# Pads in three tile pools move transposed activations and inner feed-forward tiles to 224 modulo 256 bytes

## The chip, the cores and the metric

The kernel runs on one core of one Trainium2 chip. The metric is the device time of one execution in microseconds (us), given as a median over runs. Where a time comes from the profile, it is from one profiled execution, and its times count from the start of its span.

## The reference

The program is two transformer stacks of two layers each, one after the other, on 512 tokens with 1024 features (the first stack has 256 context tokens besides). All of it is in float32. Cut to what takes the time:

```python
def sq_relu_mlp(h, w1, w2):                       # first stack, 1024 -> 4096 -> 1024
    return jnp.square(jax.nn.relu(h @ w1)) @ w2
...
def swiglu_half(x, w1, w3, w2):                   # second stack, 1024 -> 2816 -> 1024
    return 0.5 * ((jax.nn.silu(x @ w1) * (x @ w3)) @ w2)
...
    for layer in range(DEPTH):                    # first stack
        y_c, y_l = ab_mixer(...) if layer % 2 == 0 else c_mixer(...)
        x = x + mod_l[:, :, 2] * y_l
        x = x + mod_l[:, :, 5] * sq_relu_mlp(modulate(x, norm2_g[layer], mod_l, 3), mlp_w1[layer], mlp_w2[layer])
...
    for l in range(DEPTH):                        # second stack
        x = layer_norm(ALPHA * x + swiglu_half(x, ffn1_w1[l], ffn1_w3[l], ffn1_w2[l]), ln1_g[l], ln1_b[l])
        h = x @ w_in[l]
        mix = jnp.concatenate([out_a, out_b, out_c], axis=-1) @ w_out[l]
        x = layer_norm(ALPHA * x + mix, ln2_g[l], ln2_b[l])
        x = layer_norm(ALPHA * x + swiglu_half(x, ffn2_w1[l], ffn2_w3[l], ffn2_w2[l]), ln3_g[l], ln3_b[l])
```

`ab_mixer`, `c_mixer` and the three branches `out_a`, `out_b`, `out_c` are attention and recurrences; they begin and end with dense products over 1024 features.

## The kernel before

Every dense product is made of three matmuls (`mm3`, line 154): operands are split into a high and a low part (names ending in H and L, or `wh` and `wl` for weights), and high by high, high by low and low by high are added up in PSUM. Each of them goes through `mm` (line 142). A matmul has a moving operand, whose columns stream through the array, and a stationary one of 128 columns, which a weight load puts there before. In a row of the profile `ps<-hH,wh` the first name after the arrow is the moving operand and the second the stationary one; `128*128 128x512` is the shape of the stationary operand and that of the output.

There are three patterns of product.

- Activations move over stationary weights, 8 row blocks and 24 matmuls for each 128 output features. This is `genA` (line 1624), the first product of `mlp` (line 1151) and that of `ffn` (line 1823). The moving tiles are `hH`, `hL` (512 tokens) and in the first stack `hcH`, `hcL` (256 context tokens): activations transposed to features by tokens. At the start of each feed-forward the first pieces run on 256 tokens at a time. Outside the mixers this makes, by the loops, 3840 matmuls of 512 columns in the four feed-forwards of the second stack (22 feature tiles by 2 weights by 24, less four tiles that run in halves) and 1440 in the two of the first.
- Weights move over stationary activations: `genB` (line 1638) and `genP` (line 497) in the mixers, with `hH`, `hL`, `hcH`, `hcL` as the stationary tiles.
- Weights move over stationary inner tiles of a feed-forward: `genP` in `mlp` with the tiles called `hid`, and `gen2` (line 1797) in `ffn` with `hidH`, `hidL`.

Weights come by DMA into `wf` (two buffers of 1 MB), are split by ScalarE (`wh`) and VectorE (`wl`) into four buffers each, one piece ahead of use, and used in the order of the list `specs`. In the feed-forwards nothing else stands on TensorE's queue but transposes of `x`; in the mixers generators of small work are woven between the dense matmuls by a rough clock (`service`, `drive`), and this order does not know where a tile lies.

Tiles are laid out from two ends of each partition. `pool` (line 193) opens a pool on the left, on top of what is open there; `right` (line 190) does it on the right. On the left lie `const`, then `hT` (`hH`, `hL`), then `sm1` (small tiles of the first stack) with `hTc` (`hcH`, `hcL`) and the pools of layer and feed-forward above it; for the second stack `sm2` takes the place of `sm1`, with `hidf` (`sl`, `hidH`, `hidL`) above. The weight buffers lie on the right. In the built program the tiles start at these bytes of a partition:

| tiles | byte before | mod 256 | mod 512 |
|---|---|---|---|
| `wh`, `wl` (all buffers) | 180192 and up, 4096 apart | 224 | 480 |
| `hH`, `hL` | 21952, 38336 | 192 | 448 |
| `hcH`, `hcL` | 62752, 70944 | 32 | 288 |
| `hid` of `mlp` | 87328 and up, 3072 apart | 32 | 288 |
| `hidH`, `hidL` of `ffn` | 69344 and up, 2048 apart | 224 | 224 |
| `kTH`, `kTL`, `vH`, `vL`, `pt` of the first stack's layer 1 | 82208, 88352, 94496, 100640, 134432 and up | 32 | 288 |

A matmul of 512 columns takes a slice that starts a multiple of 512 bytes further on, so the residues are those of the operands too. Only the pieces of weights that are 272 or 288 columns wide have slices at other residues.

Of the kernel before, what the change touches and what calls it, by code (L numbers as in the profile page):

```python
# [7 lines left out]
F32 = mybir.dt.float32  # L8
# [4 lines left out]
PSUM = bass.MemoryType.PSUM  # L13
# [11 lines left out]
VF = 1.0  # L25
# order of emission in the mixers: priorities of chains, backlog they may see, order of the projections
MIX = {"lim": 12.0, "marg": 0.15, "slow": "", "ord": "UVQZ", "invy": (5, 8, 10, 12, 14) + tuple(range(16, 31)), "invw": 6.0, "rgw": 0, "rgp": 1,
# [6 lines left out]
PVX = 1  # L34
N6, NQ, N5, N5B = 9, 4, 13, 15


# [10 lines left out]
class Lane:  # L48
    """an engine whose calls are passed on and added to a rough clock, for the order of emission"""

# [52 lines left out]
class Slots:  # L103
    """tiles handed out and given back in the order of emission"""

# [10 lines left out]
class Net:  # L116
# [10 lines left out]

# [1 line left out]
    def ps(self):  # L129
# [60 lines left out]
    def right(self, es, name, bufs=1):  # L190
        return es.enter_context(self.tc.tile_pool(name=name, bufs=bufs, side="right", reuse_waits="tile"))

    def pool(self, es, name, **kw):
        return es.enter_context(self.tc.tile_pool(name=name, bufs=1, side="left", reuse_waits="tile", **kw))

# [1 line left out]
    def run(self):  # L197
# [38 lines left out]

    # ================= first block =================
    def slots(self, pool, n, size, tag):
        return Slots([pool.tile([128, size], F32, name=f"{tag}{i}") for i in range(n)])

    def tok(self, t):
        """features by tokens of tile t: context 0, 1, latents 2..5"""
        a, i = (self.hTc, t) if t < 2 else (self.hT, t - 2)
        c = slice(i * 128, i * 128 + 128)
        return a[0][:, :, c], a[1][:, :, c]
# [12 lines left out]
    def mild(self, i):  # L258
        """pieces whose low parts GpSimd takes: all of them, or the second half of each"""
        n = len(self.specs)  # L260
        if i in SLOW0:
            self.slow |= {n, n + 1}
        if -i - 1 in SLOW0:
            self.slow |= {-n, -n - 1}
# [44 lines left out]

    # feature blocks of layer 0's projection: columns, width, pieces of modulation weights between  # L310
    L0_proj = [
# [31 lines left out]

# [1 line left out]
    def ada_setup(self):  # L345
# [9 lines left out]
        p = self.pb.get()  # L355
# [8 lines left out]
        self.pb.put(p)  # L364
        # [layer, latents or context, part of the modulation, feature block]
        self.mod = cp.tile([128, 2, 2, 6, 8], F32, name="mod")
# [19 lines left out]
    def ada_first(self, c, n, f):  # L386
        """half c of shift and scale of the first norm, two row blocks"""
        r = 64 * c
        if n == 0:
            self.abanks[c] = self.pb.get()  # L390
        for k in range(2):
            for s in range(2):
                self.nc.tensor.matmul(self.abanks[c][r + 32 * s:r + 32 * s + 32, :], lhsT=self.sT[:, 2 * n + k, :], rhs=f[:, k, s, :],
                                      start=n + k == 0, stop=n == 3 and k == 1)
                self.pe(0.43)
        if n == 3:
            self.spawn(self.ch_first(c), 0)
# [44 lines left out]
    def gate_row(self, pool, l, i, r):  # L442
        """row of modulation i (2 or 5) for all partitions"""
        t = pool.tile([128, 1024], F32, name=f"gate{l}{i}{r}")
        j0 = (i % 2) * 2
        for j in range(2):
            q = 32 * (j0 + j) + r
            self.nc.sync.dma_start(t[:, j * 512:j * 512 + 512], self.mD[l][i // 2][q].partition_broadcast(128))
        return t

    def ch_mod(self, t, x, l, i, name, tm, keep=True):
        """modulated rms norm of token tile t, by features and split; x as two halves of 512"""
        r = 1 if t < 2 else 0
# [43 lines left out]
    def genP(self, tiles, width, evac, raw=(), lhs=None, gate=None):  # L497
        """token-major product with eight row blocks of weights, token tiles by pairs"""
        if lhs is None:
# [29 lines left out]

# [1 line left out]
    def layer0(self):  # L531
# [8 lines left out]
        vH, vL = kp.tile([128, 6, 128], F32R, name="vH"), kp.tile([128, 6, 128], F32R, name="vL")  # L540
        # keys of a head above themselves, and their low parts
        kD, kL = [kp.tile([128, 768], F32R, name=f"kD{g}") for g in range(2)], kp.tile([128, 768], F32R, name="kL")
# [9 lines left out]
        aTD = self.dp.tile([12, 512], F32, name="aTD")  # L552
        # norm of the inputs while the modulation is on its way
        self.tmes = ExitStack()
# [86 lines left out]

        # -- window attention
        def ch_rope(t, qk, v):
# [170 lines left out]
        def ch_switch():  # L814
            """room for the rest once the window attention is done"""
            yield [("pv", t, g) for t in range(6) for g in range(2)]
# [4 lines left out]

        # -- mLSTM
        def ch_gate():
# [312 lines left out]
    def gated(self, x, p, g):  # L1136
        """x += g * p"""
        s = self.tms.get()
        self.tms.put(s)
        self.tt(s, p, g, ALU.mult)  # L1140
        self.tt(x, x, s, ALU.add)
# [7 lines left out]

# [1 line left out]
    def mlp(self, l):  # L1151
# [81 lines left out]

# [1 line left out]
    def layer1(self):  # L1235
# [121 lines left out]
        def ch_rl(g, t, rl):  # L1357
            """rows of the reciprocal sums, for all partitions"""
            yield [("l", g, t, j) for j in range(4)] + [("ps", 1), ("SO", 1)]
# [78 lines left out]

# [1 line left out]
    def spawn(self, gen, prio=1):  # L1440
# [70 lines left out]

# [1 line left out]
    def spec(self, parts, a, b, cut, extra=False):  # L1513
        self.specs.append((parts, a, b, cut, extra))

    def specraw(self, q):
        """pieces of the modulation weights, used as they are"""
        for l, sc, k in q:
# [11 lines left out]
    def issue(self):  # L1530
        """loads for which a buffer is free"""
        while self.nr in self.released:
# [11 lines left out]
    def wsplit(self):  # L1544
        """closures that split the next piece"""
        i = self.ns
# [44 lines left out]
    def ahead(self):  # L1591
        """queue the split of the next weights"""
        self.issue()
# [19 lines left out]
    def specA(self, w, c0, n, extra=False):  # L1613
        """columns c0..c0+n of w, output features by 128"""
        for c in range(c0, c0 + n, 256):
# [8 lines left out]
    def genA(self, n, evac, more=(), take=tuple):  # L1624
        """n pieces of up to two output tiles of 128 features, 512 tokens; evac gives the bank back"""
        m = 0
# [11 lines left out]
    def genB(self, toks, width, evac):  # L1638
        """token-major, token tiles by pairs; evac gives the bank back"""
        w = [self.flat(self.W(1)), None]  # L1640
# [17 lines left out]

    # ================= second block =================
    def second_specs(self):  # L1660
# [80 lines left out]
    def g_layer_norm(self, y, n, eps, g, b):  # L1741
        """in place (y - mean) * rsqrt(var + eps) * g + b over n columns"""
        nc, sm = self.nc, self.sm
# [14 lines left out]
    def chain_T(self, t, x):  # L1758
        """x transposed and split into the columns of tile t of hT"""
        hH, hL = self.hT  # L1760
# [36 lines left out]
    def gen2(self, hs, epi):  # L1797
        """token-major product of the hidden tiles with 1024 columns"""
        n = len(hs)
# [98 lines left out]
    def mixers(self, l):  # L1898
# [12 lines left out]

        # conv weights by feature, spatial biases by token
        raw = self.sm.tile([128, 128], F32, tag="raw", name="raw", bufs=1)
# [52 lines left out]
        v4 = lambda x: x.rearrange("p (t h s) -> p t h s", t=4, h=8)  # L1966
        # small constants of the layer
        row = lambda nm, n: self.row(cs, I[nm + "_2"][l], n, nm)
# [21 lines left out]
        def ch_gdn_gates():  # L1990
# [30 lines left out]
            yield  # L2021
            # row of the cumulated gates of the chunk for its tokens
            gT = cs.tile([32, 128], F32, name="gd_T")
# [117 lines left out]
        def ch_inv():  # L2141
# [19 lines left out]
            yield P["invw"]  # L2161
            # E for the queries: keys up to the query of the same chunk
            for c in range(2):
# [18 lines left out]
        def head_out(out, ov, gate, nh, sq_, p, ev):  # L2182
            """rms norm per head of 64 of ov (PSUM), times gate"""
            sq = v2(sq_[:, :nh * 64], nh)
# [153 lines left out]
        def ch_prep():  # L2338
            """inverses and off-diagonal blocks of a tile as diagonal blocks"""
            Lc, Tc = T["Lc"], T["Tc"]  # L2340
# [353 lines left out]
```

## Time and profile before

| | |
|---|---|
| median of 3 runs | 3851.73 us (3850.28 to 3855.07) |
| span of the profiled execution | 3851.4 us; no other time is given for it |
| TensorE busy with matmuls | 3754.8 us, 97% |
| weight loads | 3016.6 us, beside the matmuls |
| VectorE, ScalarE, GpSimd busy | 1893.6, 1316.6 and 324.7 us |
| DMA engines' share | 30.4% |

The busy share of TensorE counts a matmul until its modelled end, and matmuls overlap; how fast they follow each other is read from the starts of rows of a timeline, or from the number of matmuls in a stretch.

### The profile page before, as it was taken

To read this page: it belongs to the slowest core of one execution; us is meant where nothing else is said; L and a number is where in the kernel's file an instruction comes from. 1 tells how busy PE (TensorE), PEld (TensorE's weight loads), DVE (VectorE), ACT (ScalarE), POOL (GpSimd) and SP (SyncE) were. 2 spreads that over 40 slices of the span, in tenths; PEclk is the share of its full clock that TensorE was granted. 3 is DMA by queue.
4 is the path that set the end of the run, shared out by engine and by line. 5 is a ranking of instruction groups with operands and counts; after the bars stand their busy time and mean duration, and the time that the engine had idled before them with its cause. 6 is when DMAs were issued, how large, how long until landed. Compare 5 with 4: busy or idle time off the path is not lost.

```text
span 3851.4 us, 46517 instructions
## 1 busy us (share of the span) xinstructions
PE 3754.8 (97%) x18941; PEld 3016.6 (78%) x18941; DVE 1893.6 (49%) x3367; ACT 1316.6 (34%) x2213; POOL 324.7 (8%) x283
## 2 busy tenths in 40 slices
PE   8999899999999999999999999999999999999998
PEld 5676777777877778878888878888888888778887
DVE  4646663333368654443334586433433355864334
ACT  4547441211345532232222543222222225423221
POOL 1202200000011000000000241000000002410000
PEclk9999999999999999999999999999999999999999
DMA  6214542433221122223323421232333234212222
GB/s 241 69 50 143 170 167 99 156 99 102 66 72 57 42 91 88 91 96 99 104 83 121 103 80 66 89 103 82 99 99 104 89 116 102 77 66 93 99 88 82
DMA packets 282310, 379.65 MB, mean 99 GB/s; under 512 B 49224, under 2 KB 207296, under 8 KB 276976
## 3 DMA queue, kind: packets, MB, share of 16 engines
q1 hardware_dynamic: 282096, 376.68, 30.4%
q8 instruction: 148, 2.42, 0.3%
q14 instruction: 66, 0.54, 0.0%
HBM read 359.50 MB, written 17.15 MB: 98 GB/s over the span
## 4 chain that ended last, share of the span: by engine, by line
PE 86%; DVE 7%; ACT 2%; POOL 1%; DMA 1%; issue 1%; SPq 0%; POOLq 0%; ACTq 0%; DVEq 0%
PE ps L142 82%; PE ps L151 3%; POOL r L81 1%; PE ps L380 1%; DVE wl L81 1%; DVE x L81 1%; DVE ui L81 1%; DVE ua L81 1%; DVE hL L81 1%; DVE mx L81 0%; DMA fa<-in_ada_w_dram 0%; DVE st L81 0%; ACT wh L81 0%; DVE tm L81 0%; DVE u L81 0%
## 5 line engine op out<-in xcount | busy, mean ns | idle before, releaser
L81 ACT ACTIVATE wh<-wf 128x1024 fp32r<-128x1024 f32 (+2 forms) x516 | 538.0, 1050 | 1493.7 <-PE ps L142 1261.4
L81 DVE TENSOR_TENSOR wl<-wf,wh 128x1024 fp32r<-128x1024 f32 (+2 forms) x496 | 600.3, 1216 | 809.2 <-ACT wh L81 808.8
L142 PE MATMUL ps<-hH,wh 128*128 128x512 f32 (+1 forms) x2336 | 885.6, 380 | 6.8 <-ACT hH L81 5.6
L142 PE MATMUL ps<-hL,wh 128*128 128x512 f32 (+1 forms) x2336 | 881.8, 378 | 0.0
L142 PE MATMUL ps<-hH,wl 128*128 128x512 f32 (+1 forms) x2336 | 881.0, 377 | 0.0
L142 PEld LDWEIGHTS ps<-hH,wh 128*128 128x128 f32 x2336 | 440.0, 189 | 108.0 <-issue 9.5
L142 PEld LDWEIGHTS ps<-hL,wh 128*128 128x128 f32 x2336 | 440.8, 189 | 88.8 <-DVE ss L81 1.7
L142 PEld LDWEIGHTS ps<-hH,wl 128*128 128x128 f32 x2336 | 440.7, 189 | 88.3
L142 PE MATMUL ps<-wh,hid 128*128 128x512 f32 x1280 | 405.1, 395 | 0.0
L81 POOL TENSOR_TENSOR r<-rs,mhalf 128x1 f32<-128x1 f32 (+4 forms) x112 | 135.9, 1215 | 2775.4 <-DVE rs L81 2760.7
L142 PE MATMUL ps<-wh,hH 128*128 128x512 f32 (+3 forms) x800 | 315.3, 395 | 3.8 <-ACT uc L81 2.1
L142 PE MATMUL ps<-wh,hL 128*128 128x512 f32 (+3 forms) x800 | 303.4, 380 | 4.5 <-DVE hL L81 4.2
L142 PE MATMUL ps<-wl,hH 128*128 128x512 f32 (+3 forms) x800 | 302.3, 379 | 1.0 <-DVE wl L81 1.0
L142 PEld LDWEIGHTS ps<-wh,hid 128*128 128x128 f32 x1280 | 239.6, 187 | 58.0
L142 PE MATMUL ps<-wh,hidH 128*128 128x512 f32 x704 | 274.3, 390 | 0.0
L142 PE MATMUL ps<-wl,hidH 128*128 128x512 f32 x704 | 274.0, 389 | 0.0
L142 PE MATMUL ps<-wh,hidL 128*128 128x512 f32 x704 | 273.9, 389 | 0.0
L142 PE MATMUL ps<-wl,hid 128*128 128x512 f32 x640 | 252.5, 394 | 0.0
L81 DVE SCALAR_TENSOR_TENSOR sl<-sl,ps 128x512 f32<-128x512 f32 x88 | 60.5, 687 | 259.7 <-PE ps L142 259.6
L142 PEld LDWEIGHTS ps<-wh,hH 128*128 128x128 f32 x800 | 152.1, 190 | 43.3 <-issue 5.8
L142 PEld LDWEIGHTS ps<-wh,hL 128*128 128x128 f32 x800 | 152.3, 190 | 36.9 <-DVE hL L81 7.4
L142 PEld LDWEIGHTS ps<-wl,hH 128*128 128x128 f32 x800 | 152.7, 191 | 26.2 <-DVE wl L81 1.5
(369 smaller groups left out, 4740.7 us busy)
## 6 DMA issues: line engine op xcount, KB each, us to landing
wf<-in_ffn_w_dram SPq DMA_DIRECT2D x120, 1024.0 KB
wf<-in_mlp_w_dram SPq DMA_DIRECT2D x64, 1024.0 KB
wf<-in_ada_w_dram SPq DMA_DIRECT2D x40, 1024.0 KB
wf<-in_w_in_dram SPq DMA_DIRECT2D x24, 1024.0 KB
wf<-in_ffn_w_dram SPq DMA_DIRECT2D x24, 512.0 KB
wf<-in_ab_w_in_dram SPq DMA_DIRECT2D x10, 1024.0 KB
fa<-in_ada_w_dram SPq DMA_DIRECT2D x16, 512.0 KB
wf<-in_w_out_dram SPq DMA_DIRECT2D x16, 512.0 KB
```

The source lines that it names most:

```text
L81: r = f(*a, **kw)
L142: self.nc.tensor.matmul(out, lhsT=l, rhs=r, start=start, stop=stop)
L151: self.nc.tensor.transpose(out, in_, self.ident)
L380: self.nc.tensor.matmul(self.abank[32 * j:32 * j + 32, :], lhsT=self.sT[:, k, :], rhs=f[:, 512 * j:512 * j + 512], start=k == 0, stop=k == 7)
```

## The change

A table `PAD` names three pools; when one of them is opened, a tile of so many bytes per partition is made first, and nothing writes or reads it. The rest of the diff takes out comments and docstrings.

```diff
+PAD = {'const': 32, 'sm1': 160, 'sm2': 224}
...
     def right(self, es, name, bufs=1):
-        return es.enter_context(self.tc.tile_pool(name=name, bufs=bufs, side="right", reuse_waits="tile"))
+        p = es.enter_context(self.tc.tile_pool(name=name, bufs=bufs, side="right", reuse_waits="tile"))
+        if name in PAD:
+            p.tile([128, PAD[name] // 4], F32, name="pad" + name, bufs=1)
+        return p
 
     def pool(self, es, name, **kw):
-        return es.enter_context(self.tc.tile_pool(name=name, bufs=1, side="left", reuse_waits="tile", **kw))
+        p = es.enter_context(self.tc.tile_pool(name=name, bufs=1, side="left", reuse_waits="tile", **kw))
+        if name in PAD:
+            p.tile([128, PAD[name] // 4], F32, name="pad" + name)
+        return p
```

All three pools are on the left. In the built program the tiles then start here:

| tiles | byte after | mod 256 | mod 512 |
|---|---|---|---|
| `wh`, `wl` | as before | 224 | 480 |
| `hH`, `hL` | 21984, 38368 | 224 | 480 |
| `hcH`, `hcL` | 62944, 71136 | 224 | 480 |
| `hid` of `mlp` | 87520 and up | 224 | 480 |
| `hidH`, `hidL` of `ffn` | 69600 and up | 224 | 480 |
| `kTH`, `kTL`, `vH`, `vL`, `pt` | 82400, 88544, 94688, 100832, 134624 and up | 224 | 480 |

The large working tiles of the second stack's mixers lie on the right and stay. Each engine has the same instructions in the same order as before, and the waits are the same but for one copy on GpSimd in the first stack's window attention, which waits for VectorE alone instead of VectorE and ScalarE. No DMA is added or moved.

## Rows read from the trace of the kernel before

**Rows 1.** The page: span, engines' busy time, and shares of the last chain.

```profile
span 3851.4 us, 46517 instructions
...
PE 3754.8 (97%) x18941; PEld 3016.6 (78%) x18941; DVE 1893.6 (49%) x3367; ACT 1316.6 (34%) x2213; POOL 324.7 (8%) x283
...
PE 86%; DVE 7%; ACT 2%; POOL 1%; DMA 1%; issue 1%; SPq 0%; POOLq 0%; ACTq 0%; DVEq 0%
```

**Rows 2.** Stretches: us, then busy (count) of PE, PEld, DVE, ACT, POOL; clock, DMA.

```profile
2620.00:2670.00 50.00, 50.00 (x216) 40.27 (x215) 17.47 (x19) 14.09 (x18) 0.00 (x0) 1.00 0.31 99
...
1594.00:1634.00 40.00, 40.00 (x173) 32.08 (x172) 17.23 (x21) 7.03 (x8) 0.00 (x0) 1.00 0.25 79
...
2280.00:2340.00 60.00, 56.33 (x459) 47.18 (x458) 39.32 (x67) 29.44 (x59) 20.48 (x18) 0.97 0.19 54
```

**Rows 3.** Timeline of TensorE: start and length in us; three pairs, nine matmuls apart.

```profile
2819.82 0.40 PE L142 MATMUL ps<-hL,wh 128*128 128x512 f32 x1
...
2821.92 0.40 PE L142 MATMUL ps<-hL,wh 128*128 128x512 f32 x1
...
1334.71 0.40 PE L142 MATMUL ps<-wl,hH 128*128 128x512 f32 x1
...
1336.81 0.39 PE L142 MATMUL ps<-wl,hH 128*128 128x512 f32 x1
...
2600.03 0.39 PE L142 MATMUL ps<-wl,hidH 128*128 128x512 f32 x1
...
2602.07 0.39 PE L142 MATMUL ps<-wl,hidH 128*128 128x512 f32 x1
```

**Rows 4.** Groups of matmuls by form: xcount, busy us, mean ns, idle before.

```profile
L142 PE MATMUL ps<-hH,wh 128*128 128x512 f32 x1952 | 776.7, 398 | 0.0
...
L142 PE MATMUL ps<-wh,hid 128*128 128x512 f32 x1280 | 405.1, 395 | 0.0
...
L142 PE MATMUL ps<-wh,hidH 128*128 128x512 f32 x704 | 274.3, 390 | 0.0
...
L142 PE MATMUL ps<-wh,hH 128*128 128x512 f32 x640 | 268.2, 420 | 3.8 <-ACT uc L81 2.1 <-ACT hH L81 1.4 <-DVE vL L81 0.3
...
L142 PE MATMUL ps<-hH,wh 128*128 128x256 f32 x384 | 108.9, 289 | 6.8 <-ACT hH L81 5.6 <-ACT wh L81 1.2
...
L142 PE MATMUL ps<-hcH,wh 128*128 128x256 f32 x256 | 72.9, 285 | 0.0
```

**Rows 5.** Timeline, layer 1 attention of the first stack: two rows twelve matmuls apart.

```profile
1172.22 0.51 PE L142 MATMUL ps<-kTH,hcH 128*128 128x384 f32 x2
...
1174.30 0.34 PE L142 MATMUL ps<-kTH,hcH 128*128 128x384 f32 x1
```

**Rows 6.** Timeline after three breaks in the stream: pairs eight, four and four matmuls apart.

```profile
3150.66 0.40 PE L142 MATMUL ps<-wl,hidH 128*128 128x512 f32 x1
...
3152.51 0.39 PE L142 MATMUL ps<-wh,hidH 128*128 128x512 f32 x1
...
3156.71 0.48 PE L142 MATMUL ps<-wh,hidH 128*128 128x512 f32 x1
...
3157.71 0.39 PE L142 MATMUL ps<-wl,hidH 128*128 128x512 f32 x1
...
1223.35 0.71 PE L142 MATMUL ps<-pt,vH 128*128 128x512 f32 x2
...
1224.35 0.33 PE L142 MATMUL ps<-kTH,hcL 128*128 128x384 f32 x1
```

**Rows 7.** Timeline, layer 0's feed-forward, context tokens: two pairs, 22 matmuls apart.

```profile
573.63 0.28 PE L142 MATMUL ps<-hcL,wh 128*128 128x256 f32 x1
...
576.13 0.28 PE L142 MATMUL ps<-hcH,wl 128*128 128x256 f32 x1
...
583.16 0.28 PE L142 MATMUL ps<-hcL,wh 128*128 128x256 f32 x1
...
585.75 0.28 PE L142 MATMUL ps<-hcH,wl 128*128 128x256 f32 x1
```

## The prediction

> **What bounds the kernel now.** I read the page first, then stretches, then single rows. The page shows TensorE busy for 3754.8 of 3851.4 us and on 86% of the chain that ended last; the next engine, VectorE, has 49% [rows 1]. So the end is set by how fast matmuls follow each other, and an edit that changes no instruction matters only if it changes that. The table of stretches is read next, for what else could hold TensorE: in 50 us of a feed-forward's first product TensorE is busy throughout at full clock (1.00, which is the 2.4 GHz level), VectorE for 17.47 us, ScalarE for 14.09 us, and DMA engines at 0.31 [rows 2]. Nothing there is near its limit, so matmuls that follow each other 3% faster would still be fed. In the mixers it is different: in 60 us of one, TensorE idles 3.7 us and VectorE and GpSimd are busier [rows 2]; time won there can turn into waiting.
>
> The length of a matmul's row (0.39 or 0.40 us) is not its price, since the next starts before it ends. The price is the distance of starts, and the timeline gives it. Activations `hH` over weights: nine matmuls in 2.10 us, 233.3 ns each. Weights over `hH`: the same 2.10 us. Weights over `hidH`: 2.04 us, 226.7 ns each [rows 3]. Weights over `hid`: 173 matmuls in 40 us; with one row's length added for the edge, 40.39/173 is 233.5 ns [rows 2]. All four are 128 by 128 by 512 at the same clock, without a wait. What sets the fast one apart by the table of places is that both its operands start at 224 modulo 256; in the others one of the two is at 224 and the other at 192 or 32. Which operand moves is not it by itself: weights move in the fast stream and in two slow ones.
>
> **The change part by part.** It adds no instruction, DMA or queue entry, and drops one wait of a GpSimd copy. What moves is the start of operands. After it `hH`, `hL`, `hcH`, `hcL` and `hid` stand at 224 like the weights, and `hidH`, `hidL` stay there. If equal residues are what makes 226.7 ns, each 512-column matmul of the slow patterns gains 6.6 ns. The sum, pattern by pattern:
>
> (a) Activations over weights outside the mixers: 3840 and 1440 by the loops, 5280 of the 3 x 1952 matmuls of that form [rows 4]. Weights over `hid`: 1280 rows, and half as many with the low weights, 1920. Together 7200 x 6.6 ns = 47.5 us. They run back to back, but after each break in the stream the distance needs some matmuls to settle: in the fast pattern eight matmuls after a break took 1.85 us, 231 ns each [rows 6]. There are some fifty such restarts in the first stack's feed-forwards (after each product of modulation weights and each change to 256 columns), at 8 x 4.6 ns each: 2 us off. 45.5 us.
>
> (b) In the mixers: 576 matmuls of activations over weights (5856 less 5280), and 3 x 640 of weights over `hH` [rows 4] with 384 over `hcH`: 2880. All of it at 6.6 ns would be 19 us, none of it 0. Small products are woven between them, so many run within eight matmuls of a break, where a good half of the difference is not yet there: half at 6.6 ns and half at 2 ns is 12.4 us. Some is given back where TensorE then waits for VectorE or ScalarE. I take 8 us.
>
> (c) 256-column matmuls: 3 x 384 over `hH` and 3 x 256 over `hcH` [rows 4], 1920. Here the trace has two levels at one and the same pair of residues (32 and 224): 22 matmuls in 2.50 us, 113.6 ns, and 22 in 2.59 us, 117.7 ns [rows 7]. So at this width the state of the stream decides too, and equal residues may give the lower level, the present one, or another some 2 ns above it. Bounds: 8 us gained, 4 us lost. I take 3 us gained.
>
> Sum: 45.5 + 8 + 3 = 56.5 us, so 3851.4 becomes 3795 us; the median of the runs, 3851.7, lies 0.3 us from the profiled span, so it moves alike. Bounds of this case: 47.5 + 19 + 8 = 74.5 us gained gives 3777; 45.5 + 0 - 4 gives 3810.
>
> Costs I put at nothing: the writers of the moved tiles (ScalarE and VectorE), which have room beside 50 us of TensorE [rows 2], so that even a few per cent more on each write would show only in the mixers; and the dropped wait, off TensorE's queue.
>
> [...] First the rows: in 50 us TensorE's weight loads take 40.27 us beside 50.00 us of matmuls [rows 2], so the next weights are being read nearly all the time that a moving operand is. [...]
>
> **The rivals.** *No change:* the fast stream is fast for another reason, say the order in which `gen2` goes through eight PSUM banks, three matmuls on each. Then every pattern keeps its distance: 3851 us. For it: in rows of 512 columns only this one program pattern runs at 226.7 ns for long. Against it: a stream from quite another place. In layer 1's attention twelve matmuls of 384 columns, both operands at 32, took 2.08 us, 173.3 ns each [rows 5]. From there to 226.7 ns is 53.4 ns for 128 columns more, 0.417 ns a column, one cycle of 2.4 GHz; both then have the same 13.3 ns on top of their columns, and 233.3 ns has 20. Equal residues gave the same small remainder in both. [...]
>
> *Slower:* what is good is not equality modulo 256 but a distance of 256 modulo 512. Before, `hidH` and `hidL` stand at 224 modulo 512 and the weights at 480; after, everything stands at 480. Then the slow patterns stay where they are, and `gen2`, 3 x 704 matmuls [rows 4], falls back to 233.3 ns: 2112 x 6.6 = 13.9 us, 3865 us. For it: in the trace of before, no long stream of 512 columns has both operands at the same residue modulo 512. Against it: the 384-column stream has (288 and 288), with the small remainder; and a 512-column stream at 288 and 288 restarts like `gen2`: four matmuls after a break take 1.00 us in both [rows 6]. It decides from the point where the feed-forwards' second products show over 230 ns.
>
> *Half of it:* the state needs weights as the moving operand, as in `gen2`. Then only `hid` (1920) and the mixers' weight-moving products gain, 12.7 us and about 6 us: 3833 us. Against it, again the 384-column stream, in which keys move and no weights.
>
> That something else becomes the bound I leave out as a case: DMA at 0.31 and VectorE at a third in the dense stretch [rows 2] would have to grow threefold.
>
> **How the numbers follow.** Equal residues help everywhere: 0.77, at 3777 to 3810, likeliest 3795. Half of it: 0.05, 3833. No change: 0.10, 3851. Slower: 0.08, 3865. The range goes from 3777 to 3835 and so holds the first two, 0.82. A measurement of this kernel can tell about 0.2%, 8 us, from no change. Faster by more than that: 0.82; within it: 0.10; slower: 0.08.
>
> **What would show it.** Right: in the profile after, nine matmuls of `hH` over weights take 2.04 us instead of 2.10 in the second stack's feed-forwards, likewise weights over `hid`, and `gen2` keeps 2.04; a feed-forward's first product of 528 matmuls takes 528 x 226.7 ns, 119.7 us, instead of 123; counts, order and clock are the same. Step (b) is right if the mixers together shorten by 6 to 12 us and TensorE's idle time there grows by a few. Step (c) is right if 22 matmuls of 256 columns take 2.50 us in most places. The prediction is wrong if the distance stays at 233.3 ns with both operands at 224, if `gen2` rises to 233, or if streams of equal residue settle at a third value.

## The result and the profile after

The changed kernel takes 3806.39 us (median of 4 runs, 3803.82 to 3811.38) and the kernel before 3851.19 us (4 runs, 3850.28 to 3855.07): ratio 0.9883, 95% interval 0.9869 to 0.9897. That is 44.8 us faster; 56.5 us were forecast, and the time lies in the range.

The page of the kernel after answers to [rows 1]: span, busy times, shares of the last chain. Its profiled execution is the slowest of the four runs.

```profile
span 3809.7 us, 46516 instructions
...
PE 3707.1 (97%) x18941; PEld 3024.2 (79%) x18941; DVE 1896.2 (50%) x3367; ACT 1316.9 (35%) x2213; POOL 325.8 (9%) x283
...
PE 85%; DVE 8%; ACT 2%; POOL 2%; issue 1%; DMA 1%; SPq 0%; POOLq 0%; DVEq 0%; ACTq 0%
```

The work is the same: 18941 matmuls, and the other engines' busy times have hardly moved. TensorE is busy for 47.7 us less, and it is still what the end waits for, on 85% of the last chain.

Three stretches of the kernel after begin at the same matmuls as those of [rows 2] (columns as there).

```profile
2595.03:2645.03 50.00, 50.00 (x222) 41.44 (x221) 17.64 (x20) 14.42 (x19) 0.00 (x0) 1.00 0.33 101
1581.90:1621.90 40.00, 40.00 (x178) 33.13 (x177) 17.97 (x22) 7.16 (x8) 0.00 (x0) 1.00 0.25 79
2258.36:2318.36 60.00, 55.79 (x457) 46.96 (x456) 40.61 (x68) 29.59 (x59) 21.33 (x18) 0.97 0.21 59
```

In the first two, 222 matmuls stand where 216 stood (activations over weights) and 178 where 173 stood (weights over `hid`), at the same clock, 1.00. In the mixer's 60 us there are 457 instead of 459, and TensorE idles 4.2 us instead of 3.7: no gain in this window.

The timeline of the kernel after shows the same pairs as [rows 3], nine matmuls apart, then the first pair of [rows 6], eight apart, and last the two pairs of [rows 7], 22 apart.

```profile
2791.89 0.39 PE L146 MATMUL ps<-hL,wh 128*128 128x512 f32 x1
...
2793.93 0.39 PE L146 MATMUL ps<-hL,wh 128*128 128x512 f32 x1
...
1330.22 0.39 PE L146 MATMUL ps<-wl,hH 128*128 128x512 f32 x1
...
1332.26 0.39 PE L146 MATMUL ps<-wl,hH 128*128 128x512 f32 x1
...
2575.53 0.39 PE L146 MATMUL ps<-wl,hidH 128*128 128x512 f32 x1
...
2577.57 0.39 PE L146 MATMUL ps<-wl,hidH 128*128 128x512 f32 x1
...
3116.46 0.40 PE L146 MATMUL ps<-wl,hidH 128*128 128x512 f32 x1
...
3118.28 0.39 PE L146 MATMUL ps<-wh,hidH 128*128 128x512 f32 x1
...
578.05 0.28 PE L146 MATMUL ps<-hcL,wh 128*128 128x256 f32 x1
...
580.69 0.28 PE L146 MATMUL ps<-hcH,wl 128*128 128x256 f32 x1
...
587.59 0.28 PE L146 MATMUL ps<-hcL,wh 128*128 128x256 f32 x1
...
590.22 0.28 PE L146 MATMUL ps<-hcH,wl 128*128 128x256 f32 x1
```

Activations over weights and weights over `hH` now take 2.04 us for nine, 226.7 ns each, where they took 2.10; the second product of the second stack keeps its 2.04. The last two pairs, of 256 columns, took 2.50 and 2.59 us, and now both take 2.63 to 2.64 us, 120 ns each: this width became slower.

To see where the 44.8 us lie, the distances from the start of each dense matmul to the start of the next matmul of any kind were added up over the whole trace of before, of the kernel after, and of a second profiled run of it (last column, the run `after_again` below). A mixer is counted from its first dense matmul to the first one of the feed-forward behind it.

| us | before | after | again |
|---|---|---|---|
| 512 columns, all feed-forwards (9311) | 2164.3 | 2117.9 | 2118.0 |
| 256 columns, all feed-forwards (1728) | 216.8 | 222.0 | 221.8 |
| 512 columns, mixers (2880) | 740.1 | 733.1 | 733.9 |
| 256 columns, mixers (384) | 46.3 | 47.0 | 47.0 |
| layer 0's mixer as a whole | 481.7 | 484.6 | 484.3 |
| layer 1's mixer as a whole | 247.9 | 247.3 | 243.6 |
| the two mixers of the second stack as a whole | 628.8 | 625.8 | 625.1 |

### The profile page after: what moved, and what is told of

It reads as the page before. It is cut to its first block, busy times and chain, and to the rows that moved or that the text cites. A ratio compares the mean times of both kernels' runs of the same rounds, so it can differ in the third digit from the quotient of the medians.

```text
span 3809.7 us, 46516 instructions
## 1 busy us (share of the span) xinstructions
PE 3707.1 (97%) x18941; PEld 3024.2 (79%) x18941; DVE 1896.2 (50%) x3367; ACT 1316.9 (35%) x2213; POOL 325.8 (9%) x283
## 4 chain that ended last, share of the span: by engine, by line
PE 85%; DVE 8%; ACT 2%; POOL 2%; issue 1%; DMA 1%; SPq 0%; POOLq 0%; DVEq 0%; ACTq 0%
PE ps L146 81%; PE ps L155 3%; POOL r L85 1%; DVE ui L85 1%; DVE wl L85 1%; PE ps L390 1%; DVE x L85 1%; DVE ua L85 1%; DVE hL L85 1%; DVE mx L85 0%; DVE u L85 0%; DMA fa<-in_ada_w_dram 0%; DVE st L85 0%; DVE tm L85 0%; ACT wh L85 0%
## 5 line engine op out<-in xcount | busy, mean ns | idle before, releaser
L146 PE MATMUL ps<-hH,wh 128*128 128x512 f32 (+1 forms) x2336 | 874.8, 375 | 7.0 <-ACT hH L85 5.6
L146 PE MATMUL ps<-hL,wh 128*128 128x512 f32 (+1 forms) x2336 | 871.2, 373 | 0.3 <-DVE hL L85 0.3
L146 PE MATMUL ps<-hH,wl 128*128 128x512 f32 (+1 forms) x2336 | 870.6, 373 | 0.0
```

The source lines that it names most:

```text
L146: self.nc.tensor.matmul(out, lhsT=l, rhs=r, start=start, stop=stop)
```

## The experiments

All are the changed kernel with another table `PAD`, and nothing else differs. "Difference" is the byte at which the moving operand starts less that of the stationary one, modulo 256. Mean distances leave out starts over 250 ns apart (130 ns at 256 columns). Eight of the twelve ran once, with a profile; the kernel before took 3848.05 to 3853.69 us in the single runs beside them.

**The weights come to the activations.** Instead of `hH` the weights move, to 192, where `hH` was before; `hidH` stays at 224 and `hid` at 32.

```diff
-PAD = {'const': 32, 'sm1': 160, 'sm2': 224}
+PAD = {'wf': 32}
```

> No pad on the left; one pad of 32 bytes on the right moves the weight buffers to 192 modulo 256, where hH and hL lie in the kernel before; hid stays at 32, hidH and hidL at 224. Theory 1 (what counts is that both operands have the same residue): activations over weights now at 226.7 ns, though neither is at 224, and gen2, which no longer matches, at about 233 ns; some 5800 x 6.6 ns gained and 2112 x 6.6 ns lost, part of the first in the mixers given back: about 3826 us. Theory 2 (it is the place 224 itself that is fast): nothing at 226.7 ns any more, 3865 us. Theory 3 (it is the pattern of gen2): gen2 stays at 226.7 ns and the rest at 233.3 ns, 3851 us.

3824.34 us, as the first theory had it. A stretch of `hH` over weights (us, TensorE's busy us and matmuls, clock, DMA share, GB/s):

```profile
2602.00:2702.00 100.00, 100.00 (x442) 1.00 0.31 98
```

442 matmuls in 100 us; the kernel before has 430 in 100 us of the same product, and the changed one 443. The mean distance of `hH` over weights is 227.0 ns with both at 192, and `gen2`, whose operands now stand at 192 and 224, has risen from 226.7 to 233.3 ns. So 224 is no special place; what counts is that the two are equal.

One part of `gen2` did not rise, and it is the closest comparison here. The table of places gives one place for all weight buffers, but the pieces marked `extra` in `specs` go to a pool `wx` on the left, above `hidH` and `hidL`, and share their residue in every run: 384 of the 2112 matmuls of `gen2`. At its end `gen2` goes through twelve matmuls with these weights and twelve with the others in turn. The timeline of this run has such blocks; the first two rows have both operands at 224, the last two weights at 192, and each pair is nine matmuls apart:

```profile
1882.91 0.39 PE L146 MATMUL ps<-wh,hidL 128*128 128x512 f32 x1
...
1884.95 0.39 PE L146 MATMUL ps<-wh,hidL 128*128 128x512 f32 x1
...
1885.41 0.40 PE L146 MATMUL ps<-wl,hidH 128*128 128x512 f32 x1
...
1887.51 0.40 PE L146 MATMUL ps<-wl,hidH 128*128 128x512 f32 x1
```

2.04 us against 2.10 us within 5 us, in one product, with the same shapes. In this run the equal blocks are on average at 226.6 to 227.4 ns from their sixth matmul on, and the unequal ones are slow from their first. In the other runs with unequal weights the same blocks have means of 227.2 to 230.3 ns. The figures of `gen2` here and below are those of the weights outside `wx`.

**Differences other than 0.** Six runs put other differences under the three large patterns.

```diff
-PAD = {'const': 32, 'sm1': 160, 'sm2': 224}
+PAD = {'const': 96, 'sm1': 192, 'hid': 32, 'sm2': 160, 'hidf': 96}
```

> Pads set unequal residues: moving less stationary, modulo 256, is 64 for hH over weights, 96 for hcH over weights, 128 for weights over hid, 160 for weights over hidH. Theory 1 in its narrow form (only equal residues are fast): all of them at 233.3 ns with 512 columns, gen2 too, 3865 us. Theory 1 in its wide form (a conflict of two reads that depends on the distance): some distance comes out at 226.7 ns or another value, a lower one not excluded; 256-column matmuls show levels of their own, 113 to 120 ns. Theory 3 (gen2's pattern): gen2 stays at 226.7 ns.

3836.88 us. `hH` over weights at difference 64:

```profile
2610.00:2710.00 100.00, 100.00 (x439) 1.00 0.30 95
```

439 in 100 us, 229.0 ns: neither of the two levels known so far, so the narrow form (one slow level, 3865 us) falls.

```diff
+PAD = {'const': 160, 'sm1': 192, 'hid': 128, 'sm2': 96, 'hidf': 224}
```

> As the run before with other distances, moving less stationary modulo 256: 128 for hH over weights, 160 for hcH over weights, 224 for weights over hid, 32 for weights over hidH. Narrow form of theory 1: 233.3 ns everywhere, 3865 us. Wide form: a distance of 128 has the best chance of a level of its own, since it is half the period; a level below 226.7 ns on hH alone would bring 3865 - 5280 x 0.0066 = 3830 us or less.

3856.55 us; 232.6 ns for `hH` over weights at difference 128: a level of its own, but no fast one.

```diff
+PAD = {'const': 128, 'sm1': 192, 'hid': 64, 'sm2': 128, 'hidf': 64}
```

> As the two runs before, moving less stationary modulo 256: 96 for hH over weights, 128 for hcH over weights, 64 for weights over hid, 192 for weights over hidH. Narrow form of theory 1: 233.3 ns everywhere, 3865 us. Wide form: the distances 64 and 128 give in other patterns the price they gave in the runs before, and which operand moves does not matter.

3860.50 us; 233.3 ns for `hH` over weights at difference 96, 230.2 ns for weights over `hid` at 64.

```diff
+PAD = {'const': 192, 'sm1': 192, 'hid': 224, 'sm2': 64, 'hidf': 192}
```

> The left tiles are moved so that the start of the moving operand less that of the stationary one, modulo 256, is 160 for hH over weights, 192 for hcH over weights, 96 for weights over hid, 64 for weights over hidH. Theory 1 (a graded map: the distance of starts belongs to this difference alone, whichever tiles make it): 512 columns at 234 ns for hH over weights (difference 160 as in the run where gen2 had it), 233.4 ns for weights over hid (96), 229 to 230 ns for weights over hidH (64); 256 columns of hcH over weights near 114.4 ns (192, the lowest level seen so far, then with weights over hH). Sum against the changed kernel: 5280 x 7.3 ns + 1920 x 6.7 + 2112 x 3 - 768 x 5.3 ns = 54 us more, 3855 to 3865 us. Theory 2 (only equality matters, every other difference is the same 233.3 ns): gen2 at 233.3 too, and hcH over weights at 117 to 118 ns; 3865 to 3870 us. Theory 3 (which tiles, or which operand moves, matters besides): the distances differ from those that other tiles had at the same difference by over 2 ns.

3869.40 us, the slowest of all kernels here and 4.4 us above the first theory's range. `hH` over weights at difference 160:

```profile
2632.00:2732.00 100.00, 100.00 (x428) 1.00 0.30 95
```

428 in 100 us, 234.2 ns; `gen2` at 64 has 229.2 ns and weights over `hid` at 96 have 233.3 ns, as forecast; 256 columns of `hcH` at 192 have 115.8 ns where 114.4 was forecast. So the distances at 512 columns are the first theory's and the time is not; the first context matmuls of [rows 7] come at 580.5 us, the latest of all traces (568.5 at the earliest), and layer 0 up to there varies without any change to it, as `hid_only` shows below.

```diff
+PAD = {'const': 64, 'sm1': 160, 'hid': 64, 'sm2': 192, 'hidf': 128}
```

> Differences modulo 256: 32 for hH and hcH over weights, 160 for weights over hid, 128 for weights over hidH. Theory 1 (graded map by the difference alone): 512 columns at 233.3 ns for hH over weights (as gen2 had at 32), 234 ns for weights over hid, 232.5 ns for gen2; 256 columns of hH and hcH over weights 116.9 ns, as weights over hH had at 32. Sum against the changed kernel: 5280 x 6.6 + 1920 x 7.3 + 2112 x 5.8 - 1920 x 3 ns = 55 us more, 3855 to 3865 us. Theory 2 (only equality matters): all 512-column streams at 233.3 ns, hardly another time. Theory 3 (tiles or the moving side matter besides): distances over 2 ns away from those named.

3859.28 us, 233.3, 234.2 and 232.6 ns for the three patterns; 116.8 and 117.0 ns at 256 columns. As the first theory had it.

```diff
+PAD = {'const': 224, 'sm1': 32, 'hid': 160, 'sm2': 32, 'hidf': 160}
```

> Differences modulo 256: 192 for hH over weights, 64 for hcH over weights, 32 for weights over hid, 96 for weights over hidH. Theory 1 (graded map by the difference alone): 512 columns at 233.3 ns in hH over weights, weights over hid and gen2; 256 columns of hH over weights at 114.4 ns, of hcH over weights at 116.8 ns. Sum against the changed kernel: (5280 + 1920 + 2112) x 6.7 ns - 1152 x 5.3 - 768 x 3 ns = 54 us more, 3855 to 3865 us. Theory 2 (only equality matters): the same at 512 columns, but one level of 117 to 118 ns for all of 256 columns. Theory 3 (tiles or the moving side matter besides): distances over 2 ns away from those named.

3861.70 us; 233.3, 233.3 and 233.6 ns at 512 columns, 114.7 and 116.8 ns at 256. The mean of 114.7 hides two levels. The timeline has both at one difference (192), in the first pieces of two feed-forwards of the second stack; all 23 matmuls from the first row of a pair to the second have the same operand addresses in both:

```profile
3495.55 0.28 PE L146 MATMUL ps<-hL,wh 128*128 128x256 f32 x1
...
3498.04 0.28 PE L146 MATMUL ps<-hH,wl 128*128 128x256 f32 x1
...
2437.59 0.28 PE L146 MATMUL ps<-hL,wh 128*128 128x256 f32 x1
...
2440.18 0.28 PE L146 MATMUL ps<-hH,wl 128*128 128x256 f32 x1
```

22 matmuls take 2.49 us and 2.59 us, 113.3 and 117.7 ns each, nearly as in [rows 7] at another difference. At this width the places do not settle the level by themselves, and a mean can mix two levels.

All runs together, the mean distance in ns by difference, at 512 columns for the three large patterns, at 256 for `hH` and `hcH` over weights (`low_weights_apart`, below, is left out); where several runs or patterns had one difference, their lowest and highest:

| difference | 0 | 32 | 64 | 96 | 128 | 160 | 192 | 224 |
|---|---|---|---|---|---|---|---|---|
| 512 columns | 226.7 to 227.1 | 233.3 to 233.4 | 229.0 to 230.2 | 233.3 to 233.6 | 232.6 to 232.7 | 234.1 to 234.2 | 233.3 | 233.3 |
| 256 columns | 119.7 to 119.8 | 116.8 to 117.0 | 116.8 to 117.7 | 119.6 to 119.9 | 118.8 | 118.0 to 118.5 | 114.7 to 116.5 | 118.3 |

At 512 columns each entry is within 1.2 ns whichever tiles make it and whether weights or activations move. No other difference is as fast as 0 there; at 256 columns 0 is among the slowest.

**The changed kernel once more.** No edit.

> The changed kernel once more, as it is. Theory 1 (the 1.2 GHz stretches of layer 0's mixer, 44 us of rows in the changed kernel's trace against 34 before, come and go from run to run): they differ again, and the time lies at 3800 to 3811 us with them. Theory 2 (they belong to the changed layout): again some 44 us of them in layer 0's mixer, which takes 531 us again instead of 527. Either way matmuls of 512 columns follow at 226.7 ns and those of 256 columns at 120 ns.

The records of the granted clock in the traces of before and after have two shares alone, 1.0 and 0.5. The 1.2 GHz stretches of the expectation are those at half clock, 0.5; the 2.4 GHz level of the prediction is the full clock. In GHz both are an estimate from the price of a column, taken as one cycle: 0.417 ns at the full clock, by [rows 3] and [rows 5], and 0.833 ns at the half clock, where in the trace of before six matmuls of weights over `hH` take 2.56 us (3349.24 to 3351.80 us), 426.7 ns each for 512 columns.

3807.90 us (4 runs, 3804.00 to 3812.47); before, 13 runs beside it, 3850.80 us; ratio 0.9889, interval 0.9874 to 0.9904. The dense streams of the feed-forwards repeat to 0.2 us (table above). Layer 0 does not. Up to the context matmuls at which [rows 7] begin, some 45 us into its feed-forward, it takes until 575.8 us, with 51 us at the half clock by those records; in the profiled run after it was 577.9 us with 44, and before 573.5 us with 34. It is later than before again, so this run by itself tells little between the two theories; the run `hid_only` below tells more.

**The two parts alone.** First `hH`, `hL`:

```diff
+PAD = {'const': 32, 'sm1': 224, 'sm2': 224}
```

> One part of the change alone: hH and hL move to 224; hcH, hcL and hid stay at 32 as before, hidH at 224. Theory 1 (each pattern gains by its own residues, and the parts add up): 5280 matmuls of hH over weights at 6.6 ns are 34.8 us, 1 us off for restarts, and 256 columns of hH lose 1 to 2 us; with little from the mixers 3815 to 3822 us. Theory 2 (the parts act on each other, by the writers or the order of reads): more than 5 us off that.

3815.08 us (4 runs, 3812.04 to 3817.27); ratio 0.9907, 0.9890 to 0.9923. Then `hid`:

```diff
+PAD = {'hid': 192}
```

> The other part alone: only hid of the first stack's feed-forwards moves, from 32 to 224; hH, hL stay at 192, hcH, hcL at 32, hidH at 224. Theory 1 (the parts add up): 1920 matmuls at 6.6 ns, 12.7 us, less 0.5 to 1 us for restarts: 3838 to 3842 us, and weights over hid at 226.7 ns. Theory 2: more than 5 us off that.

3841.08 us (10 runs, 3835.69 to 3844.59); ratio 0.9974, 0.9965 to 0.9983. Both are where the first theory put them. The parts gain 35.7 and 9.7 us, 45.4 us together; the whole change gained 42.9 us beside them. In the feed-forwards' 512-column matmuls alone the gains are 33.8 us (5280 matmuls, 6.4 ns each) and 12.0 us (1920, 6.2 ns each).

`hid_only` also says something on layer 0. Up to the context matmuls at which [rows 7] begin, no operand of a matmul has another place than in the kernel before; only `hid` moved, whose products come later. First the kernel before, then `hid_only`, from the start to about there (columns as in [rows 2], the clock third from the end):

```profile
0.00:573.00 573.00, 527.54 (x2681) 383.76 (x2682) 326.90 (x898) 291.75 (x689) 102.83 (x101) 0.97 0.42 141
```

```profile
0.00:576.50 576.50, 530.73 (x2683) 385.54 (x2684) 327.15 (x898) 291.97 (x689) 104.33 (x101) 0.96 0.41 140
```

The same products with the same operand places end at 576.6 instead of 573.5 us, 3.1 us later, at a mean clock of 0.96 instead of 0.97. Over all traces here that stretch ends between 568.5 and 580.5 us, with 24 us at the half clock in the one that ends first and 48 in the one that ends last. So a few microseconds of layer 0 come and go without any change to it, and the 4.4 us that it lost up to there in the profiled run after need no cause in the layout.

**Context tiles at another place.** Since 0 is bad at 256 columns and 192 the best, `hcH` and `hcL` go to 160 and the rest stays at 224.

```diff
+PAD = {'const': 32, 'sm1': 96, 'hid': 64, 'sm2': 224}
```

> As the changed kernel, but hcH, hcL (with them layer 1's kTH, vH) start at 160 instead of 224; hH, hid, hidH stay at 224. Theory 1 (graded map by the difference of starts): 768 matmuls of 256 columns, hcH over weights at difference 192, go from 119.7 ns to about 115 ns, 3.6 us; 384 of weights over hcH at 64 go from 226.7 to about 229.5 ns, 1.1 us the other way; in all 2 to 3 us faster than the changed kernel, about 3804 us. Theory 2 (equality is best at every width, and the 120 ns of 256 columns have another reason): hcH over weights stays at 119 to 120 ns or rises, and the kernel is 1 to 3 us slower than the changed one.

3801.64 us (4 runs, 3797.57 to 3802.93), ratio 0.9871, interval 0.9856 to 0.9885. It is the fastest kernel here: all four runs lie below all eight of the changed kernel, though the two intervals against before overlap. The 22 matmuls of [rows 7] in its timeline:

```profile
573.92 0.28 PE L146 MATMUL ps<-hcL,wh 128*128 128x256 f32 x1
...
576.51 0.28 PE L146 MATMUL ps<-hcH,wl 128*128 128x256 f32 x1
```

2.59 us instead of 2.64. The mean is 116.5 ns, not the 115 forecast, instead of 119.7 in the changed kernel; over the 768 matmuls that is 2.5 us. These are shown; the rest of the 5 to 6 us to the changed kernel is not taken apart. Layer 0 up to [rows 7] ends at 573.8 us here, 4.1 and 2.0 us earlier than in the changed kernel's two profiled runs, and varies by as much.

**Low weights apart from high ones.** Here two of three matmuls have equal operands and the third has not.

```diff
+PAD = {'wf': 32, 'wh': 160, 'wl': 64}
```

> The left side lies as before the change (hH, hL at 192, hid at 32, hidH at 224); the high weights go to 192 and the low ones to 32. In a product of hH, hL over weights the order of matmuls is hH over wh, hL over wh, hH over wl, so that of three matmuls two have their own two operands at equal places and the third has a difference of 160. Theory 1 (what counts is the moving operand against the stationary operand that is loaded next, while it streams): the matmul before the one over wl takes long, that is hL over wh to the next start is some 240 ns or more in a steady stretch, and hH over wl is followed after 226 to 227 ns. Theory 2 (what counts is a matmul's own two operands): hH over wl is followed after 234 ns or more, the other two after 226.7 ns. Theory 3 (a stream locks in as a whole): all three at one distance, and not a mean of 226.7, 226.7 and 234, 229.1 ns, but 233 ns or more. By theories 1 and 2 the mean over three is 229.1 ns and the whole, from the run with all weights at 192 (3824 us): plus 5280 / 3 x 7.3 ns, less 704 x 4 ns in the second products of the second stack and 640 x 7.5 ns in those of the first, 3827 to 3832 us; by theory 3 3845 us.

3859.81 us: the third theory's direction, and 15 us above its price, which is not fully taken apart. Against `weights_to_192`, from which the price was worked out, weights over `hH` in the mixers took 231.5 instead of 229.3 ns, and layer 0 up to [rows 7] ended at 575.0 instead of 569.0 us. The timeline of `hH`, `hL` over weights:

```profile
2700.27 0.40 PE L146 MATMUL ps<-hH,wh 128*128 128x512 f32 x1
2700.51 0.40 PE L146 MATMUL ps<-hL,wh 128*128 128x512 f32 x1
2700.74 0.40 PE L146 MATMUL ps<-hH,wl 128*128 128x512 f32 x1
2700.97 0.39 PE L146 MATMUL ps<-hH,wh 128*128 128x512 f32 x1
...
2702.37 0.40 PE L146 MATMUL ps<-hH,wh 128*128 128x512 f32 x1
```

Nine matmuls take 2.10 us again. By position the means are 233.3 ns from `hH` over `wh`, 231.7 from `hL` over `wh`, 232.7 from `hH` over `wl`: 232.6 on average, where 229.1 would be the mean of a pair-by-pair price. No place in the three keeps the fast distance, also not the ones whose own operands and whose next weights are at equal places. One unequal operand in three takes the fast state from the whole stream. The blocks of `gen2` in `weights_to_192` fit this: there it took up to five equal matmuls in a row to be back at the fast distance, and here never more than two stand together.

## Why the prediction was right, and where its sum was off

**The bound and the mechanism held.** Only distances of matmuls changed, no engine took TensorE's place, and equal places gave 226.7 ns in all three patterns. A feed-forward's first product of 528 matmuls, forecast at 119.7 us, takes 119.7.

**Step (a)**, 45.5 us forecast for the 512-column matmuls of the feed-forwards: 2164.3 less 2117.9 is 46.4 us, 46.3 in the second profile. Of the 47.5 us without restarts these took about 1 us, not the 2 allowed: eight matmuls after a break take 1.82 us.

**Step (b)**, 8 us forecast in the mixers: as a whole they went from 1358.4 to 1357.7 and 1353.0 us, 0.7 and 5.4 us, not the 6 to 12 that the prediction named as its sign. The matmuls themselves did nearly what was worked out. At the full clock 1239 of them, with eight or more dense ones right before, gained 6.1 ns each, and some 1270 nearer to a break 2.2 ns each: 10.4 us where "half at 6.6 ns and half at 2 ns" gave 12.4. The term that was mis-sized is what is given back, 4.4 us in the forecast and 9.7 and 4.9 in the two profiles. A large part of it lies in layer 0's mixer, which took 2.9 and 2.6 us more, with 37 and 48 us at the half clock (0.5) where it had 31 before, and in the first profile TensorE's idle time over the whole kernel grew from 96.6 to 102.6 us (96.9 in the second).

**Step (c) is mis-sized in sign too.** 3 us gained were forecast for 256 columns; in the profile after, 5.2 us were lost in the feed-forwards and 0.7 us in the mixers. The step held "another level some 2 ns above" possible and gave it 4 us as a bound. That level is what came: 119.7 ns where `hcH` over weights had 116.8 (768 matmuls) and 119.8 where `hH` over weights had 118.3 (1152), 3.9 us, which is the bound. The rest of the 5.9 us is in matmuls that these means leave out: 192 that move weights, and those after a break or at the half clock. Equal places give the same 13.3 ns on top of the columns at 256 as at 512 columns (at 0.417 ns a column 256 columns are 106.7 ns, 512 are 213.3), and at 256 that is no gain, since unequal places cost 8 to 13 ns there. The prediction had worked out the 13.3 ns itself from 384 and 512 columns [rows 5]; put to 256 columns it gives 120 ns.

Together, 46.4 gained in (a), 0.7 in the mixers and 5.2 lost at 256 columns are 41.9 us, and the profiled span shortened by 41.7; in the second profile 46.3, 5.4 and 5.0 lost are 46.7 of 47.2 us. The medians' 44.8 us lie between. That the time came out within the range is not luck: the term that carries it, (a), was right to 1 us, and the miss of 11.7 us is (b) and (c).

**The rivals.** *No change* falls: the distance went with the places in every run, and `gen2`'s order of banks did not protect it when the weights moved away. The runs show that where one operand starts against the other is worth up to 7.5 ns of each matmul of 512 columns (226.7 ns at 0, 234.2 at 160). *Slower* falls: `gen2` stayed at 226.7 ns at a distance of 0, as it was at 256 modulo 512, so these tiles show no difference between the two. The trace of before held a sign of it that the prediction passed over: in `gen2`'s 384 matmuls with weights in `wx` both operands stood at 224 modulo 512, and they followed at 226.9 ns, the others at 226.8. *Half of it* falls: activations over weights gained as much for each matmul as weights over `hid`, 6.4 and 6.2 ns with restarts.

**Open** is what in the chip makes the difference. The last experiment and the blocks in `weights_to_192` speak against a price that each pair of operands pays by itself, and for a rhythm that a stream falls into after some equal matmuls and loses at an unequal one; what keeps it, no run here shows. All differences tried with the large patterns are multiples of 32 bytes; smaller steps are open. Open too is whether the changed layout has a little more time at the half clock: the mean clocks of its eight runs are 0.988 to 0.991, those of before 0.989 to 0.992. The longest run of each is at 0.988 (3812.47 us) and 0.989 (3857.14 us), the shortest at 0.991 (3803.82 us) and 0.992 (3847.76 us).

## What to carry to other kernels

When TensorE is dense, read the distance of starts for each pattern, not the busy time of a row, and compare it between patterns with equal shape: a difference of 3% without any wait (233.3 ns against 226.7 here) can lie in where the buffers start. Place moving and stationary operands at the same residue modulo 256 where 512 columns stream for long (226.7 to 227.1 ns here, 229.0 to 234.2 at every other difference tried), and all buffers of one stream alike, since one that is off in every three matmuls took the gain from its neighbours (232.6 ns on average). Look at narrower matmuls apart, because at 256 columns the same placement cost time (119.7 and 119.8 ns against 116.8 and 118.3 before).

## What the runs showed of the hardware that was not expected

- The distance at 512 columns depends on the difference of starts in steps: 226.7 ns at 0, 229 to 230 at 64, 232.6 at 128, 233.3 at 32, 96, 192 and 224, 234.2 at 160, whichever operand moves.
- At 256 columns the order is another: 114.7 to 116.5 ns at 192, 120 at 0; and there two levels (113.3 and 117.7 ns) were seen with the same operand addresses in one execution.
- A stream in which one of three matmuls has unequal operands runs at 231.7 to 233.3 ns throughout, while twelve equal ones between twelve unequal ones were at 226.6 to 227.4 ns from the sixth on.
